# Row numbers through TensorE in two bf16 parts, an earlier scatter, and splits held at the ends of stages, in a two-block fp32 model on one Trainium2 core

## Chip, cores and metric

The kernel runs on one core of one Trainium2 chip. The metric is the device time of one execution in microseconds; lower is better.

## The reference

256 tokens of width 1024, batch 1, all in fp32. The first block has two layers: each a mixer (mLSTM in layer 0, stick-breaking attention in layer 1) and a PEER FFN. A vector c gives, through six matrices per layer (`ada_w`), shift, scale and gate of the mixer and of the FFN. The second block has two layers of half-FFN, attention (MLA, then FOX), half-FFN, and a gated per-layer embedding (PLE).

```python
def first_block(...):
    for layer in range(2):
        sh1, sc1, g1, sh2, sc2, g2 = split(silu(c) @ ada_w[layer] + ada_b[layer], 6)
        h = rmsnorm(x, norm_mix_g[layer]) * (1 + sc1) + sh1
        x = x + g1 * mixer(h)                      # mLSTM | stick-breaking
        h = rmsnorm(x, norm_ffn_g[layer]) * (1 + sc2) + sh2
        x = x + g2 * peer_ffn(h)

def peer_ffn(xb):                                  # 16384 experts, 8 heads, top 16
    s = q(xb) @ sub_keys                           # two lists of 128 scores per head
    s_top, i_top = top_k(s, 16)
    g_top, pos = top_k(s_top[0] + s_top[1], 16)
    expert = (i_top[0] * 128 + i_top[1])[pos]
    act = gelu(dot(peer_u[expert], x))
    return sum(softmax(g_top) * act * peer_v[expert])

def second_block(...):
    for i in range(2):
        h = h + 0.5 * swiglu(rms_norm(h, g_ffn1[i]))
        h = h + attention(rms_norm(h, g_mix[i]))   # MLA | FOX
        h = h + 0.5 * swiglu(rms_norm(h, g_ffn2[i]))
        h = h + sigmoid(rms_norm(h, g_ple[i]) @ w_gate) * (p[i] @ w_proj)
```

## The kernel before

The ten stages follow one another: mLSTM, PEER of layer 0, stick-breaking, PEER of layer 1, FFN, MLA, FFN with PLE, FFN, FOX, FFN with PLE. Weights come from HBM as 1 MB tiles `raw` on SyncE's queue (SP), four of them in flight. For exact fp32 products most weights are split: ScalarE (ACT) rounds a high part `whi` (L228), VectorE (DVE) subtracts it to give `wlo` (L229), and TensorE (PE) does three passes, high×high, low×high, high×low (L277 to L279, L243 to L245). The activations are split alike when the transposes of the next stage's input leave PSUM: `xhi` on ACT, `xlo` on DVE (L320, L321 in `split_T`; L331, L332 with a shift). `split` honours a list `holds`: an entry is a tuple of instructions behind which the next split must stand on the same engine (`issue_after`, an edge in the order, on one engine). A scheduler orders the instructions of each engine by priorities, apart from blocks under `pe_order`, where PE's order is that of the code.

`ada_first` makes the first shift and scale before anything else can run. For the shift, four tiles of `ada_w` go through fp32 matmuls with one output row (L591; each passes twice); the row is turned into columns by eight transposes of one column (L600) and `sh1` is added up (L601). For the scale, four further tiles go through DVE (`ada_scale`, L499), then eight transposes (L517) and sums on ACT (L524). The loads of both alternate.

`peer` serves the first tokens (80 in layer 0, 96 in layer 1) by gathers and the others densely. Dense: `u_phase` multiplies 128 blocks of 1 MB (two experts' rows of 128) of `peer_u` with the tokens (L1443), ACT applies Gelu into X (L1445), a matrix of gates G is built by one-hot products (L1477) and multiplied into X on DVE (L1483), and `v_phase` sums with `peer_v` (L1494). Each of both has two halves of 32 tiles: u0, u1, v0, v1. Gathered: `route` finds the top 16 of 8 heads for 128 tokens; `scatter` spreads the row numbers (`sidx`) and gates (`sg`) to one per partition by four fp32 matmuls with a spreading matrix (L1343), masked products and sums on DVE (L1347, L1349). Then for every four columns one fp32 matmul with the identity carries four row numbers through PE (L1387, held behind the last u or v matmul), ACT casts them to integers (L1389), and GpSimd (POOL) issues one indirect DMA of 128 rows (0.5 MB) per column. DVE takes the dot product (L1399) or adds the weighted row to `sacc` (L1416). The later modulation matrices (`extra`) come in between as ada rows of 0.5 MB and are summed on DVE (L483); at the end a matmul turns a sum into columns (L517, shift or scale) or spreads it (L548, gate `g2b`, after the bias is added on DVE, L546). `par` mixes these generators with the u or v tiles by counts; `route` takes all 16 top-16 steps of the second token block in its turn, so the scheduler may put them ahead of the scatter on DVE.

`last` ends `peer`: per column half two matmuls with `back` bring `sacc` home (L1531), four transposes bring the dense part `oT` (L1534), `residual` multiplies by the gate and adds to x on DVE (L467, L468), and `head` transposes x for the next stage (L303). Attention (`attend`) runs eight head pairs: logits (L928 to L931), exp on ACT (L944), products.

```python
c0, c1, c2 = nf * 27 // 160, nf * 44 // 160, nf * 46 // 160
ne = 14 if l == 0 else 3
par(u0, 12, (rt, 18))
par(u0, half - 12, (rt, 24), (f, c0), (extra, ne))
```

## Time and profile before

| | us |
|---|---|
| median of 3 runs | 2836.63 (2835.41 to 2844.22) |
| profiled execution | 2841.97 |
| its span | 2839.8 |
| PE busy in it | 2740.8 (97%) |
| DVE, ACT, POOL busy | 1938.5 (68%), 929.6 (33%), 450.9 (16%) |
| mean granted PE clock | 0.986 |

The two PEER stages take 177 to 906 and 1064 to 1741 us, more than half of the span. The u and v matmuls alone are busy 604.6 and 608.0 us. A "busy" PE is one with a matmul in flight, at whichever clock; idle time stands with the engine that waits and names what ended the wait.

### The profile page before, as it was taken

Reading aid. Unit: us, or ns where it says so; the run is one execution under the profiler, and the core shown is the slowest. Engines: PE = TensorE matmul, PEld = TensorE weight load, DVE = VectorE, ACT = ScalarE, POOL = GpSimd, SP = SyncE. Lnnn points to the kernel's source line nnn. Section 1 sums busy time; section 2 is a strip of 40 time slices with the busy share of each in tenths; the row PEclk is TensorE's granted clock in tenths of the full one; section 3 lists DMA queues with packets and bytes.
Section 4 is the critical chain, followed back from the end, with each engine's and each line's share of the span. In section 5 each row is a group of like instructions: output and inputs, shape, how many; then the busy total and the mean of one; then the engine's idle time right before and its main releaser. Section 6 shows DMA issues by size and latency. Waiting matters only on the chain.

```text
span 2839.8 us, 47705 instructions
## 1 busy us (share of the span) xinstructions
PE 2740.8 (97%) x19226; PEld 2544.7 (90%) x19226; DVE 1938.5 (68%) x4021; ACT 929.6 (33%) x1730; POOL 450.9 (16%) x445
## 2 busy tenths in 40 slices
PE   7999999999998999999999998999999999999999
PEld 4789989999998779999999987998799989877997
DVE  6778756767645978857777545667766666676665
ACT  4752111100000654111100002446654554456544
POOL 0000332333432000133344431000000000000000
PEclk9999999999999999999999999999999999999999
DMA  7655998999998634799999996554245555452553
GB/s 294 226 179 174 364 372 331 389 359 373 396 407 333 227 118 142 289 401 415 408 408 405 409 409 258 193 186 153 94 169 188 182 179 190 153 175 93 193 191 110
DMA packets 155580, 747.90 MB, mean 263 GB/s; under 512 B 15696, under 2 KB 17360, under 8 KB 111840
## 3 DMA queue, kind: packets, MB, share of 16 engines
q1 hardware_dynamic: 93984, 527.93, 49.9%
q0 software_dynamic: 58752, 213.94, 19.4%
q8 instruction: 151, 2.47, 0.4%
q10 hardware_dynamic: 2624, 3.00, 0.3%
q14 instruction: 69, 0.57, 0.1%
HBM read 743.76 MB, written 1.05 MB: 262 GB/s over the span
## 4 chain that ended last, share of the span: by engine, by line
PE 85%; DMA 7%; DVE 5%; ACT 2%; issue 1%; POOL 0%; SPq 0%; DVEq 0%; ACTq 0%; POOLq 0%
PE ps_acc L1494 17%; PE ps_mm L1443 17%; PE ps_mm L277 7%; PE ps_mm L279 7%; PE ps_mm L278 7%; DMA raw<-in_peer_v_dram 4%; PE ps_acc L244 4%; PE ps_acc L243 4%; PE ps_acc L245 4%; PE ps_acc L1149 3%; PE ps_acc L1151 3%; PE ps_acc L1150 3%; PE ps_mm L1477 1%; DMA raw<-in_ada_w_dram 1%; DVE wlo L229 1%
## 5 line engine op out<-in xcount | busy, mean ns | idle before, releaser
L229 DVE TENSOR_TENSOR wlo<-raw,whi 128x1024 fp32r<-128x1024 f32 (+1 forms) x440 | 532.6, 1214 | 243.4 <-ACT whi L228 232.7
L228 ACT CAST whi<-raw 128x1024 fp32r<-128x1024 f32 (+1 forms) x440 | 456.2, 1042 | 512.2 <-PE ps_mm L278 241.9
L1494 PE MATMUL ps_acc<-X,raw 128*128 128x176 f32 (+1 forms) x4096 | 608.0, 309 | 11.0 <-DMA raw<-in_peer_v_dram 10.8
L1443 PE MATMUL ps_mm<-hT,raw 128*128 128x176 f32 (+1 forms) x4096 | 604.6, 308 | 2.4 <-ACT jT L1673 2.4
L1494 PEld LDWEIGHTS ps_acc<-X,raw 128*128 128x128 f32 x4096 | 587.0, 191 | 16.2 <-DMA raw<-in_peer_v_dram 16.1
L1443 PEld LDWEIGHTS ps_mm<-hT,raw 128*128 128x128 f32 x4096 | 588.6, 191 | 3.4 <-ACT jT L1673 2.6
L277 PE MATMUL ps_mm<-xhi,whi 128*128 128x256 f32 (+1 forms) x1488 | 418.3, 283 | 7.4 <-ACT xhi L332 5.1
L278 PE MATMUL ps_mm<-xlo,whi 128*128 128x256 f32 (+1 forms) x1488 | 418.2, 282 | 3.3 <-DVE xlo L321 3.0
L279 PE MATMUL ps_mm<-xhi,wlo 128*128 128x256 f32 (+1 forms) x1488 | 417.9, 281 | 0.0
L1416 DVE SCALAR_TENSOR_TENSOR sacc<-row,dots,sacc 128x1024 f32<-128x1024 f32 x172 | 220.7, 1283 | 117.2 <-DMA row<-in_peer_v_dram,ix 116.2
L1399 DVE SCALAR_TENSOR_TENSOR row<-row,hn 128x1024 f32<-128x1024 f32 x176 | 213.1, 1224 | 114.7 <-DMA row<-in_peer_un_dram,ix 114.3
L277 PEld LDWEIGHTS ps_mm<-xhi,whi 128*128 128x128 f32 (+1 forms) x1488 | 279.6, 189 | 11.9 <-ACT xhi L332 5.3
L278 PEld LDWEIGHTS ps_mm<-xlo,whi 128*128 128x128 f32 (+1 forms) x1488 | 280.0, 188 | 7.3 <-DVE xlo L321 3.5
L279 PEld LDWEIGHTS ps_mm<-xhi,wlo 128*128 128x128 f32 (+1 forms) x1488 | 281.2, 189 | 0.5 <-DVE wlo L229 0.3
L1392 POOL DMA_INDIRECT row<-in_peer_un_dram,ix x176 | 209.9, 1192 | 446.7 <-ACT ix L1389 156.1
L1392 POOL DMA_INDIRECT row<-in_peer_v_dram,ix x176 | 197.2, 1120 | 340.2 <-ACT ix L1389 177.5
L1445 ACT ACTIVATE X<-ps_mm 128x352 f32<-128x352 f32 (+1 forms) x128 | 57.6, 450 | 495.5 <-PE ps_mm L1443 495.5
L1389 ACT CAST ix<-ps_mm 128x4 int32<-128x4 f32 x88 | 14.2, 161 | 511.8 <-PE ps_mm L1387 440.8
L1483 DVE SCALAR_TENSOR_TENSOR X<-ps_mm,X 128x128 f32<-128x128 f32 (+1 forms) x210 | 66.1, 365 | 125.2 <-PE ps_mm L1477 122.0
L1149 PE MATMUL ps_acc<-whi,ah 128*128 128x512 f32 x352 | 139.4, 396 | 0.0
L1151 PE MATMUL ps_acc<-whi,al 128*128 128x512 f32 x352 | 137.6, 392 | 0.0
L1150 PE MATMUL ps_acc<-wlo,ah 128*128 128x512 f32 x352 | 137.0, 389 | 0.0
(467 smaller groups left out, 3795.1 us busy)
## 6 DMA issues: line engine op xcount, KB each, us to landing
raw<-in_ffn_dram SPq DMA_DIRECT2D x132, 1024.0 KB, 4.8
raw<-in_peer_u_dram SPq DMA_DIRECT2D x128, 1024.0 KB, 7.9
raw<-in_peer_v_dram SPq DMA_DIRECT2D x128, 1024.0 KB, 11.3
raw<-in_ada_w_dram SPq DMA_DIRECT2D x28, 1024.0 KB, 5.4
row<-in_ada_w_dram POOLq DMA_DIRECT2D x40, 512.0 KB, 10.9
raw<-in_peer_wq_dram SPq DMA_DIRECT2D x16, 1024.0 KB, 4.8
raw<-in_fox_in_dram SPq DMA_DIRECT2D x12, 1024.0 KB, 5.1
raw<-in_ma_vo_dram SPq DMA_DIRECT2D x8, 1024.0 KB, 5.6
```

The costliest lines, as they stand in the source:

```text
L228: nc.scalar.copy(hi[:, 0:u], raw)
L229: nc.vector.tensor_sub(lo[:, 0:u], raw, hi[:, 0:u])
L277: nc.tensor.matmul(o, wh, xh[:, k, :], start=(k == 0), stop=False)
L278: nc.tensor.matmul(o, wh, xl[:, k, :], start=False, stop=False)
L279: self.last_mm = nc.tensor.matmul(o, wl, xh[:, k, :], start=False, stop=(k == NK - 1))
L1149: nc.tensor.matmul(o, ah[:, t], wh[:, n], start=(c == 0), stop=False)
L1150: nc.tensor.matmul(o, ah[:, t], wl[:, n], start=False, stop=False)
L1151: nc.tensor.matmul(o, al[:, t], wh[:, n], start=False, stop=(c == FFC - 1))
L1392: nc.gpsimd.indirect_dma_start(row, None, src, bass.IndirectOffsetOnAxis(held["ix"][:, k:k + 1], 0))
L1416: nc.vector.scalar_tensor_tensor(sacc[u], row, w, sacc[u], OP.mult, OP.add)
L1443: self.last_mm = nc.tensor.matmul(ps[:, i * TD:(i + 1) * TD], raw[:, o:o + P], hT[:, k, TS:S], start=(k == 0), stop=(k == NK - 1))
L1494: self.last_mm = nc.tensor.matmul(o, w, xs[:, 0, :], start=(first and c % 2 == 0), stop=last, skip_group_check=True)
```

## The change

In words: (1) `ada_first` sums the scale on PE as well: 16 further fp32 matmuls, all four tiles of the shift loaded first, then four of the scale; DVE's seven sums, the eight 128-column transposes and ACT's sums go. (2) `scatter` carries row number in two parts (row and column of the expert grid) and the gate in one 384-column matmul per unit, two in all; the parts are kept in bf16, and each index pass is two bf16 matmuls that add up in PSUM. (3) The top-16 steps of the second token block stand behind the scatter on DVE; the scatter comes after 7 tiles of u0, held ahead of the next tile's first matmul; u0 takes 33 of 160 gathered columns instead of 27, the later phases fewer, and ada rows go 6, 16, 16, 16 (layer 0) and 0, 3, 3, 3 (layer 1) instead of 14 and 3 in each. (4) `last` transposes `oT` ahead of the `back` matmuls and calls `head` for both halves at the end. (5) `boundary` sets `holds` at the end of every stage with a next one: the first `free` splits behind the last residual add, further ones behind the last evacuation; in `attend` five splits are held behind the exp of head pairs 1 to 5.

```diff
+    def boundary(self):
+        if self.gain is not None:
+            self.holds = [] if self.free == 5 else [(self.add_ins,)] * self.free + [self.evac_ins] * (5 - self.free)
...
@@ ada_first @@
-        scale = self.ada_scale(self.I["ada_w"][0, :, D:2 * D], self.col("ada_b0", 8, 8), self.col("norm_mix_g0"), m["a1"])
+        for e in range(2):
+            for k0 in range(0, NK, 2):
...
+                        nc.tensor.matmul(row[2 * e + h][0:1, :], self.cs[:, k:k + 1], raw[:, o:o + 512], start=(k == 0),
+                                         stop=(k == NK - 1))
...
+                (nc.vector.tensor_copy if h else nc.scalar.copy)(t[0:1, :], row[2 * e + h][0:1, :])
...
@@ mlstm @@
-            self.holds = [(self.sum_ins, self.scale_ins)]
+            self.holds = [(self.tsp_ins,), self.evac_ins, self.evac_ins]
...
@@ attend @@
+            if p in (2, 3, 4, 5, 6):
+                self.holds.append((ex,))
...
@@ peer: tops, scatter @@
+                    with ExitStack() as hold:
+                        if tb:
+                            hold.enter_context(self.tc.issue_after(scattered[-1].ins))
+                        self.top16(rp, s_sb[tb][:, c, :], tv[tb][:, c, :], ti[tb][:, c, :])
...
+                e = rp.tile([P, 3, P], F32, name=f"ex_{l}")
+                nc.scalar.copy(e[:, 2, :], g)
+                nc.vector.tensor_scalar(e[:, 0, :], s0, float(P), float(l * P * P), OP.mult, OP.add)
+                nc.scalar.copy(e[:, 1, :], s1)
...
+                    spread_mm.append(nc.tensor.matmul(ps[:, 0:3 * P], spread[:, u, :], e.rearrange("p a b -> p (a b)"),
+                                                      start=True, stop=True))
...
+                    scattered.append(nc.vector.tensor_reduce(s3[:, :, o:o + n], t4, AX.X, OP.add))
+                    nc.scalar.copy(sidx[:, :, o:o + n], s3[:, 0:2, o:o + n])
...
-                            nc.tensor.matmul(ps[:, 0:PACE], self.ident, sidx[:, col:col + PACE], start=True, stop=True)
+                            for a in range(2):
+                                nc.tensor.matmul(ps[:, 0:PACE], self.identb, sidx[:, a, col:col + PACE],
+                                                 start=(a == 0), stop=(a == 1))
...
+                                if g == 0 and spread_mm and i + k == 0:
+                                    hold.enter_context(self.tc.issue_after(spread_mm[-1].ins))
...
@@ last @@
-                            if tb == 0:
-                                for u in range(2):
-                                    nc.tensor.matmul(ps, back[:, u, :], sacc[u][:, nh * 512:(nh + 1) * 512], start=(u == 0),
-                                                     stop=False, skip_group_check=True)
...
+                            for u in range(0 if tb else 2):
+                                nc.tensor.matmul(ps, back[:, u, :], sacc[u][:, nh * 512:(nh + 1) * 512], start=False,
+                                                 stop=(u == 1), skip_group_check=True)
...
-                        if self.gain is not None:
-                            self.head(nh)
+                    if self.gain is not None:
+                        self.head(0)
+                        self.head(1)
+                        self.boundary()
...
-            c0, c1, c2 = nf * 27 // 160, nf * 44 // 160, nf * 46 // 160
-            ne = 14 if l == 0 else 3
-            par(u0, 12, (rt, 18))
-            par(u0, half - 12, (rt, 24), (f, c0), (extra, ne))
+            c0, c1, c2 = nf * 33 // 160, nf * 43 // 160, nf * 44 // 160
+            ne = 16 if l == 0 else 3
+            par(u0, 7, (rt, 15))
+            next(u0)
+            par(u0, half - 8, (rt, 28), (f, c0), (extra, 6 if l == 0 else 0))
```

`boundary` is called at the end of `tail`, `lin_m` (when `late` is not set) and `last`; `free` is 2 for MLA and FOX, 5 for the FFN ahead of a PLE, 1 elsewhere.

PE in u0 of layer 0, before, around the scatter (L1343) and the first index matmul (L1387); a row with x16 is one tile of `peer_u`, and the first one here is the tenth:

```order
L1443 MATMUL ps_mm_2635<-hT_1607,raw_2636 128x176 x16
L1343 MATMUL ps_mm_2657<-ex_2655,spread_1603 128x128
L1343 MATMUL ps_mm_2666<-r_g_2495,spread_1603 128x128
L1443 MATMUL ps_mm_2687<-hT_1607,raw_2688 128x176 x11
L1343 MATMUL ps_mm_2657<-ex_2655,spread_1603 128x128
L1443 MATMUL ps_mm_2687<-hT_1607,raw_2688 128x176 x5
L1443 MATMUL ps_mm_2719<-hT_1607,raw_2720 128x176 x7
L1343 MATMUL ps_mm_2666<-r_g_2495,spread_1603 128x128
L1443 MATMUL ps_mm_2719<-hT_1607,raw_2720 128x176 x9
L1387 MATMUL ps_mm_2763<-sidx_1562,consts 128x4
```

And with the change (the first row is the seventh tile; L1360 is the scatter, L1408 an index pass):

```order
L1468 MATMUL ps_mm_2575<-hT_1612,raw_2576 128x176 x16
L1360 MATMUL ps_mm_2604<-ex_2600,spread_1608 128x384
L1360 MATMUL ps_mm_2610<-ex_2600,spread_1608 128x384
L1468 MATMUL ps_mm_2616<-hT_1612,raw_2617 128x176 x16
L1408 LDWEIGHTS cb
L1408 MATMUL ps_mm_2648<-sidx_1567,cb 128x4
L1408 LDWEIGHTS cb
L1408 MATMUL ps_mm_2648<-sidx_1567,cb 128x4
```

The four matmuls that stood within tiles ten to twelve are two ahead of the eighth, and the first index pass follows the eighth tile instead of the twelfth. Two to three tiles lie between one index pass and the next in both.

DVE at the end of layer 1's PEER, before, from the copy of the dense sum `oT` on:

```order
L1524 COPY oT_13997<-ps_acc_11877 128x2x160
L229 TENSOR_TENSOR wlo_14167<-raw_14164,whi_14166 128x1024
L1416 SCALAR_TENSOR_TENSOR sacc_1_13548<-row_13974,dots_8588,sacc_1_13548 128x1024
L229 TENSOR_TENSOR wlo_14171<-raw_14164,whi_14170 128x1024
L229 TENSOR_TENSOR wlo_14237<-raw_14234,whi_14236 128x1024
L229 TENSOR_TENSOR wlo_14241<-raw_14234,whi_14240 128x1024
L229 TENSOR_TENSOR wlo_14307<-raw_14304,whi_14306 128x1024
L467 TENSOR_TENSOR tsp_14049<-ps_mm_14042,g2b 128x512
L468 TENSOR_TENSOR x_84<-x_84,tsp_14049 128x512
```

And with the change:

```order
L1549 COPY oT_14081<-ps_acc_11949 128x2x160
L1438 SCALAR_TENSOR_TENSOR sacc_1_13595<-row_14058,dots_8629,sacc_1_13595 128x1024
L473 TENSOR_TENSOR tsp_14133<-ps_mm_14126,g2b 128x512
L474 TENSOR_TENSOR x_84<-x_84,tsp_14133 128x512
L473 TENSOR_TENSOR tsp_14143<-ps_mm_14138,g2b 128x512
L474 TENSOR_TENSOR x_85<-x_85,tsp_14143 128x512
L473 TENSOR_TENSOR tsp_14155<-ps_mm_14148,g2b 128x512
L474 TENSOR_TENSOR x_84<-x_84,tsp_14155 128x512
L473 TENSOR_TENSOR tsp_14165<-ps_mm_14160,g2b 128x512
L324 SCALAR_TENSOR_TENSOR xlo_14171<-ps_mm_14172,cols,xhi_14170 128x256
L474 TENSOR_TENSOR x_85<-x_85,tsp_14165 128x512
L230 TENSOR_TENSOR wlo_14251<-raw_14248,whi_14250 128x1024
```

Five `wlo` splits that stood ahead of the residual adds (L467, L468; now L473, L474) are gone from there; one stands behind the last add, the others behind rows not shown.

PE at the ada shift of layer 0 in u1, before (L1477 is the last product that DVE takes up ahead of the sum, L517 the transposing matmuls):

```order
L1477 MATMUL ps_mm_3796<-B_3740,A_3738 128x64
L1477 LDWEIGHTS A_3738
L1477 MATMUL ps_mm_3796<-B_3740,A_3738 128x64
L1387 MATMUL ps_mm_3814<-sidx_1562,consts 128x4
L517 MATMUL ps_mm_3822<-consts,ada_3283 128x128 x4
L517 MATMUL ps_mm_3828<-consts,ada_3283 128x128 x4
```

And with the change (L1502, L528):

```order
L1502 MATMUL ps_mm_4438<-B_4382,A_4380 128x64
L1408 LDWEIGHTS cb
L1408 MATMUL ps_mm_4456<-sidx_1567,cb 128x4
L1408 LDWEIGHTS cb
L1408 MATMUL ps_mm_4456<-sidx_1567,cb 128x4
L1468 MATMUL ps_mm_4467<-hT_1612,raw_4468 128x176 x16
L528 MATMUL ps_mm_4491<-consts,ada_3782 128x128 x4
L528 MATMUL ps_mm_4497<-consts,ada_3782 128x128 x4
```

One whole tile now stands between that product and the transposes.

## Rows read from the trace of the kernel before

**Rows 1.** Page, busy us (share of the span) and instructions of each engine.

```profile
PE 2740.8 (97%) x19226; PEld 2544.7 (90%) x19226; DVE 1938.5 (68%) x4021; ACT 929.6 (33%) x1730; POOL 450.9 (16%) x445
```

**Rows 2.** Waits of PE: engine, line, releaser: us in total, times, longest.

```profile
PE ps_acc L1494 <- DMA raw<-in_peer_v_dram: 10.8, 24, 2.5
...
PE ps_mm L303 <- DVE x L468: 8.1, 8, 3.0
...
PE ps_mm L548 <- DVE ada L546: 5.6, 1, 5.6
...
PE ps_mm L517 <- DVE ada L483: 4.2, 1, 4.2
PE ps_acc L928 <- ACT e L944: 3.4, 2, 3.1
...
PE ps_mm L303 <- DVE x L1215: 2.6, 1, 2.6
...
PE ps_mm L1443 <- ACT jT L1673: 2.4, 1, 2.4
```

**Rows 3.** Windows, PE: stretch, length, busy (instructions), granted clock, DMA share, GB/s.

```profile
361.10:364.60 3.50, 2.86 (x4) 0.51 1.01 407
443.10:449.90 6.80, 4.86 (x19) 0.50 0.83 291
...
1750.40:1757.20 6.80, 5.53 (x13) 0.50 0.35 145
...
2484.20:2491.10 6.90, 4.59 (x17) 0.51 0.85 302
```

**Rows 4.** Timeline of the start: start, us, engine, line, instruction, count [idle before].

```profile
8.59 5.76 PE L591 MATMUL ps_acc<-raw,cs 128*1 128x512 f32 x8 [8.59 <-ACT cs L1682]
...
21.14 7.03 PE L591 MATMUL ps_acc<-raw,cs 128*1 128x512 f32 x16 [1.65 <-DMA raw<-in_ada_w_dram]
...
30.85 1.28 DVE L499 SCALAR_TENSOR_TENSOR ada<-raw,cs,ada 128x1024 f32<-128x1024 f32 x1
...
38.40 0.79 PE L277 MATMUL ps_mm<-xhi,whi 128*128 128x256 f32 x2 [5.11 <-ACT xhi L332]
```

**Rows 5.** Timeline of layer 0's scatter and first index matmuls, PE and DVE.

```profile
278.04 0.29 DVE L1335 SCALAR_TENSOR_TENSOR ex<-r_sel,r_sel 128x128 f32<-128x128 f32 x1
...
297.38 0.28 PE L1387 MATMUL ps_mm<-sidx,consts 128*128 128x4 f32 x2
297.52 14.57 PE L1443 MATMUL ps_mm<-hT,raw 128*128 128x176 f32 x96
...
306.94 1.22 DVE L1399 SCALAR_TENSOR_TENSOR row<-row,hn 128x1024 f32<-128x1024 f32 x1
...
311.93 0.28 PE L1387 MATMUL ps_mm<-sidx,consts 128*128 128x4 f32 x2
```

**Rows 6.** Groups by line and shape: count, busy us, mean ns, idle before.

```profile
L1477 PE MATMUL ps_mm<-B,A 128*128 128x64 f16 x1344 | 55.1, 193 | 0.0
```

**Rows 7.** Timeline of DVE ahead of the ada shift's sum in u1.

```profile
440.68 0.69 DVE L1483 SCALAR_TENSOR_TENSOR X<-ps_mm,X 128x512 f32<-128x512 f32 x1 [2.92 <-PE ps_mm L1477]
...
443.62 1.27 DVE L483 SCALAR_TENSOR_TENSOR ada<-row,cs,ada 128x1024 f32<-128x1024 f32 x1
```

**Rows 8.** Window of layer 1 (columns as rows 3); page, DMA issues: count, KB, us.

```profile
1207.00:1584.00 377.00, 374.61 (x3231) 1.00 1.02 407
...
row<-in_ada_w_dram POOLq DMA_DIRECT2D x40, 512.0 KB, 10.9
```

**Rows 9.** End of layer 1's PEER: window of PE (columns as rows 3), timeline of DVE.

```profile
1741.04:1762.44 21.40, 12.24 (x56) 0.84 0.49 185
...
1744.81 4.62 DVE L229 TENSOR_TENSOR wlo<-raw,whi 128x1024 fp32r<-128x1024 f32 x4
1749.35 0.69 DVE L467 TENSOR_TENSOR tsp<-ps_mm,g2b 128x512 f32<-128x512 f32 x1
```

**Rows 10.** Timeline of DVE ahead of MLA's first exp.

```profile
1999.24 2.35 DVE L229 TENSOR_TENSOR wlo<-raw,whi 128x1024 fp32r<-128x1024 f32 x2
```

More of the change, by code (lines that the diff above doesn't have):

```diff
@@ L444, in tail @@
             self.head(1)
+            self.boundary()
     def part(self, nb, tb):
@@ L460, in add @@
             if isinstance(gate, float):
-                nc.vector.scalar_tensor_tensor(xs, ps, gate, xs, OP.mult, OP.add)
+                self.add_ins = nc.vector.scalar_tensor_tensor(xs, ps, gate, xs, OP.mult, OP.add)
             elif gate is None:
-                nc.vector.tensor_add(xs, ps, xs)
+                self.add_ins = nc.vector.tensor_add(xs, ps, xs)
             else:
@@ L531, in ada_scale @@
         yield from self.ada_sum(src, bias, sc)
-        self.scale_ins = nc.vector.scalar_tensor_tensor(out, sc, 1.0, g, OP.add, OP.mult)
+        nc.vector.scalar_tensor_tensor(out, sc, 1.0, g, OP.add, OP.mult)
         yield
@@ L577, in ada_first @@
         m = self.mod[0]
-        scale = self.ada_scale(self.I["ada_w"][0, :, D:2 * D], self.col("ada_b0", 8, 8), self.col("norm_mix_g0"), m["a1"])
-        row = [self.ps("acc") for _ in range(2)]
+        row = [self.ps("acc") for _ in range(4)]
         ctx = ExitStack()
-        pool = ctx.enter_context(self.tc.tile_pool(name="first", bufs=3, side="right", reuse_waits="tile"))
-        for k0 in range(0, NK, 2):
-            self.uid += 1
-            end = k0 == NK - 2
-            raw = (self.wpool if end else pool).tile([P, 2048], F32, tag="raw", bufs=4 if end else 3, name=f"raw_{self.uid}")
-            nc.sync.dma_start(raw.rearrange("p (k n) -> p k n", k=2),
-                              self.I["ada_w"][0, k0 * P:(k0 + 2) * P, 0:D].rearrange("(k p) n -> p k n", p=P))
-            for k in range(k0, k0 + 2):
-                for h in range(2):
-                    o = (k - k0) * D + h * 512
-                    nc.tensor.matmul(row[h][0:1, :], self.cs[:, k:k + 1], raw[:, o:o + 512], start=(k == 0),
-                                     stop=(k == NK - 1))
-            if end:
-                ps = self.ps()
-                for h in range(2):
-                    self.uid += 1
-                    t = self.spool.tile([P, 512], F32, tag="tsp", name=f"tsp_{self.uid}")
-                    nc.scalar.copy(t[0:1, :], row[h][0:1, :])
-                    for c in range(4):
-                        nc.tensor.transpose(ps[:, h * 4 + c:h * 4 + c + 1], t[0:1, c * P:(c + 1) * P], self.ident[0:1, 0:1])
-                nc.vector.tensor_add(m["sh1"], ps[:, 0:NK], self.col("ada_b0", 0, NK))
-            if k0 < 4:
-                next(scale, None)
@@ L604, in ada_first @@
-        for _ in scale:
-            pass
+        pool = ctx.enter_context(self.tc.tile_pool(name="first", bufs=4, side="right", reuse_waits="tile"))
+        for e in range(2):
+            for k0 in range(0, NK, 2):
+                self.uid += 1
+                raw = (self.wpool if e else pool).tile([P, 2048], F32, tag="raw", bufs=4, name=f"raw_{self.uid}")
+                nc.sync.dma_start(raw.rearrange("p (k n) -> p k n", k=2),
+                                  self.I["ada_w"][0, k0 * P:(k0 + 2) * P, e * D:(e + 1) * D].rearrange("(k p) n -> p k n", p=P))
+                for k in range(k0, k0 + 2):
+                    for h in range(2):
+                        o = (k - k0) * D + h * 512
+                        nc.tensor.matmul(row[2 * e + h][0:1, :], self.cs[:, k:k + 1], raw[:, o:o + 512], start=(k == 0),
+                                         stop=(k == NK - 1))
+            ps = self.ps("acc" if e else "mm")
+            for h in range(2):
+                t = pool.tile([P, 512], F32, tag=f"row{e}{h}", bufs=1, name=f"row{e}{h}")
+                (nc.vector.tensor_copy if h else nc.scalar.copy)(t[0:1, :], row[2 * e + h][0:1, :])
+                for c in range(4):
+                    nc.tensor.transpose(ps[:, h * 4 + c:h * 4 + c + 1], t[0:1, c * P:(c + 1) * P], self.ident[0:1, 0:1])
+            b = self.col("ada_b0", 8 * e, 8)
+            if e:
+                sc = self.small(NK, "adas")
+                nc.vector.tensor_add(sc, ps[:, 0:NK], b)
+                nc.vector.scalar_tensor_tensor(m["a1"], sc, 1.0, self.col("norm_mix_g0"), OP.add, OP.mult)
+            else:
+                nc.vector.tensor_add(m["sh1"], ps[:, 0:NK], b)
@@ L1329, in peer @@
             chosen = {}
+            spread_mm, scattered = [], []
             def scatter():
                 g, s0, s1 = chosen[0]
[L1334 to L1350 removed]
```

70 lines of the change are left out of this document (36 added, 34 removed).

## The prediction, made before the change had run

> **What bounds the kernel now.** I read the busy shares first: TensorE (PE) is busy 2740.8 of 2839.8 us [rows 1]. So the matmuls set the time, and a change that leaves their count almost alone can only win or lose in the 99 us in which PE stands still and in the stretches at half clock behind those stops. The waits of PE come next [rows 2]: no wait is long, the largest is 10.8 us in 24 pieces. The change must therefore be costed wait by wait. The third view, windows laid over the stretch right after a stop, shows the second half of the price [rows 3]: the granted clock stands at 0.50 for 3.5 to 6.9 us (1.2 GHz instead of 2.4), so half of the PE busy time in such a window is lost too: 1.4, 2.4, 2.8 and 2.3 us in the four windows shown.
>
> 0.3% of the time is 8.5 us; less than that I call no change.
>
> **The start.** All eight loads of the first modulation now end in PE sums: 64 matmuls instead of 32. The first eight took 5.76 us, the last sixteen 7.03 us, or 0.44 us each [rows 4]. From 8.59 us: 5.76 + 56 × 0.44 = 30.4, with the transposes that stand in between and the small chain behind (copy, eight transposes, add, scale, evacuation, cast; some 4 us) the first projection matmul starts at about 43.5 us instead of 38.40. Before, the DVE sum ended at 30.85 + 1.28 = 32.1 us [rows 4], under the loads. So **+5 us**, bounds +2 (PE goes on without the slow first matmuls) to +8. SP loads the same eight blocks ahead of the next weights; what is behind them doesn't move.
>
> **Index matmuls.** The fp32 pass costs PE the step from 297.38 to 297.52, 0.14 us [rows 5]. The nearest rows for two bf16 passes with their weight loads are the 1344 16-bit matmuls of L1477: 55.1 us, 41 ns each [rows 6]. So 0.14 - 0.08 = 0.06 us, 40 times in layer 0 and 48 times in layer 1. Layer 1 goes by DMA (below), so I count **-2 us**, bounds 0 and -5. The Trainium skill (TensorE: Matmul & The Clock Gate, section LDWEIGHTS (loading the stationary operand)) gives a weight load of 128 columns 107 ns; by that two loads would cost 0.21 us and the 88 passes 6 us more instead of less. The 41 ns for load and matmul together speak against it, since the loads overlap; the sum doesn't use it.
>
> **Scatter and gathers in layer 0.** Before, the row numbers were formed on DVE at 278.04, yet the first index matmul stood after 12 blocks of the u pass, at 297.38 [rows 5]. Blocks cost (311.93 - 297.38) / 3 = 4.85 us. The change puts the scatter after block 7 and the first index matmul after block 8: 4 × 4.85 = 19 us sooner. PE would come to the scatter at 297.38 - 5 × 4.85 = 273.1, and DVE was ready at 278.04 + 0.29; but part of the DVE work ahead of it (top-16 steps of the second token block) now stands behind it: some 25 short operations, at 0.2 to 0.29 us each (the row that forms the numbers) 5 to 7 us. So the wait is between 0 and 5.2 us; I take 1. ScalarE (ACT) now has the Gelu of the first 16 dot products in front of the exp of the second routing and of the next evacuations, so it waits there for row 16. That row's index matmul is three blocks, 14.6 us, ahead; a first row took 306.94 - 297.38 = 9.6 us [rows 5], three more some 1.5 us each. Behind ACT stand the next index cast and the evacuations; PE has two more PSUM tiles, 9.7 us, before it waits. I take 1 us, bounds 0 and 8 per layer. Together **+2 us**.
>
> **The two ada waits in layer 0.** PE waited 5.6 us for the last sum of the gate (L548) and 4.2 us for that of the shift (L517) [rows 2], and lost 1.4 and 2.4 us of clock behind them [rows 3]. Why, shows DVE: its stream waited until 440.68 for a PE product that stands right in front of L517 on PE, then had 4.2 us of work up to the end of the sum at 443.62 + 1.27 [rows 7]. In the new order the shift's matmuls stand a whole block (4.85 us) behind such a product, with nearly the same DVE operations between, some 4.6 us: the wait goes, **-6.5 us**, or nothing if rows come late. The gate's matmuls move from after block 24 to after block 36; there DVE has about 7 us to do against 4.9 of PE, so some 2 us stay: **-5 us**, bounds -7 and -1.
>
> **Layer 1.** From 1207 to 1584 the DMA engines moved 407 GB/s without a break [rows 8], and PE's waits in the v pass are all for its blocks [rows 2]. There bytes set the time. By 1207 the index groups of 20 rows are out instead of 12; a row tile is 0.5 MB [rows 8], less three ada rows that move behind: 8 × 0.5 - 1.5 = 2.5 MB, at 407 GB/s **-6 us**. Bounds: -14, if all of 10.8 and 2.4 us (the wait for jT) go; +3, if the 1.5 MB that come into the last v phase cost what they weigh (3.7 us).
>
> **Stage ends.** At the end of layer 1 PE's last v block ended at 1741.04, and the next stage's first matmul came at 1762.44; in these 21.4 us PE was busy 12.24 us, at a mean clock of 0.84 [rows 9]. DVE ran four low-part splits, 4.62 us, ahead of the residual adds [rows 9]. Now one split stands between the adds, the rest behind the last evacuation; the transposes of oT fill the wait for the last row. DVE needs 8 × 0.69 for four gated adds [rows 9]; with the last row ahead of them and transposes and xlo behind, some 3 to 4 us each, 12 to 14 us are left: **-8 us**, bounds -11 and -3. In MLA five splits (2.35 us for two [rows 10]) leave the path to the first exp and go between the head pairs, where PE was never idle; PE waited 3.4 us for exp [rows 2], with a stretch at half clock behind it like those of [rows 3]: **-5 us**, bounds -8 and -1. FOX's start: the window holds 2.3 us of standstill and 2.3 of clock [rows 3]: **-4.5 us**, bounds -7 and 0. The gate of the first PLE into the next FFN: 2.6 us [rows 2] of which the splits are part, -2.5; three further ends -1.5: **-4 us**, bounds -8 and 0. If a held split comes late instead, PE waits for wlo, 1.2 us each.
>
> **The sum:** +5 - 2 + 2 - 6.5 - 5 - 6 - 8 - 5 - 4.5 - 4 = -34 us. The profiled execution took 2841.97 us, so it would be 2808; the median of the runs is 5.3 us lower, 2836.63, which gives **2803 us**. With the bounds taken as independent its own range is 2791 to 2817.
>
> **Rivals.**
> *The chain, not the splits, sets the stage ends.* Add, square, transpose, cast follow each other, and a held split only moves behind them. Speaks for it: PE waits there for x (L468), not for a split [rows 2]. Against: the splits stand in front of that x on DVE [rows 9]. Then a third of the 21.5 us of stage ends comes: -34 + 14.5, 2817 us. Chance 0.18.
> *Layer 1 stays bound by DMA.* Blocks wait for bytes; the earlier gathers fill buffers that were full anyway, and 1.5 MB more come late: +3 instead of -6, 2812 us. For it: 407 GB/s for 377 us. Against: PE waited only 10.8 us. The Trainium skill (DMA: Bandwidth & Descriptors, section Where 436 GB/s comes from) holds that the HBM side binds at about 358 GB/s; by that rule nothing PE saves in layer 1 comes out. The trace goes past that figure for 377 us, so I don't lean on it further. Chance 0.10.
> *It doesn't do what it says.* The edges act on one engine only, and other work of DVE and ACT takes the place of the splits: stage ends -5, ada shift wait back (0), layer 1 0, start +8, row waits +4: -2 - 5 + 4 - 5 + 8 = 0, 2837 us. Chance 0.10.
> *Slower: the scatter comes before DVE is ready.* If the moved top-16 steps give DVE nothing back, PE waits 5.2 us at the scatter and loses 1.5 of clock; and if row 16 comes 18 us later than three blocks cover, ACT's held evacuations stop PE for 18 - 9.7 = 8 us and 1.5 of clock: 16 us, in each of two layers. The late rows also keep the ada waits, and layer 1 gives nothing. 32 + 8 (start) - 2 - 21.5 = +16.5, **2853 us**. It decides from about 8 us per layer on. Against it: those DVE steps do move. Chance 0.08.
>
> **The numbers.** The forecast has 0.54, the rivals 0.18, 0.10, 0.10 and 0.08. Faster by over 0.3%: 0.54 + 0.18 + 0.10 = 0.82; within: 0.10; slower: 0.08. The range 2788 to 2832 takes in the forecast with its bounds, the first two rivals and the near side of the third.
>
> **What would show it.** PE's waits for DVE ada at L559 and L528 under 3 us together; the first index matmul near 280 us; waits for x at L474 after the last v block under 3 us together; waits for e (L956) under 1 us; first L280 matmul at 42 to 46 us; DMA waits of the v pass (L1519) between 3 and 8 us. Wrong it is if PE waits at L1360 or for Gelu evacuations by more than 5 us, or if waits for wlo appear at stage starts.

## The result, and the profile after

The changed kernel takes 2854.27 us (median of 5 runs, 2852.44 to 2861.24), the kernel before 2837.10 beside it: ratio 1.0059, 95% interval 1.0041 to 1.0077. It is 17 us slower, where 34 us less were forecast. The profiled execution took 2852.44 us (span 2850.7), 10.5 us above that of before, which lies 5 us above its own median.

The page, engines (answers to [rows 1]):

```profile
PE 2754.4 (97%) x19250; PEld 2537.3 (89%) x19250; DVE 1931.0 (68%) x4005; ACT 929.4 (33%) x1728; POOL 433.2 (15%) x445
```

PE has 13.6 us more of busy time and about as much idle time as before: waits went and others came. The waits of PE (answers to [rows 2]; L559 and L528 were L548 and L517, L474 was L468):

```profile
PE ps_acc L1519 <- DMA raw<-in_peer_v_dram: 10.0, 21, 2.3
...
PE ps_mm L280 <- DVE sg L1182: 7.4, 4, 2.2
PE ps_acc L423 <- DVE rrt L422: 6.9, 2, 4.5
PE ps_mm L1360 <- ACT ex L1355: 6.5, 2, 4.6
...
PE ps_mm L1468 <- ACT jT L1700: 4.3, 1, 4.3
PE ps_mm L306 <- DVE x L474: 3.2, 5, 1.2
...
PE ps_mm L559 <- DVE ada L557: 2.2, 1, 2.2
...
PE ps_acc L938 <- ACT e L956: 1.3, 2, 0.9
...
PE ps_mm L528 <- DVE ada L494: 0.7, 2, 0.4
```

Gone are 9.8 - 2.9 = 6.9 us for ada, 4.9 for x at L474, 2.1 for the exp. New are sg and rrt (the norm of the next stage: `rrt` is its last DVE product, `sg` the first use of it in an FFN) and ex (the scatter's operand), 20.8 us together. The stretches behind the new stops, with the old gate stop first (stretch, length; busy us and instructions of PE, PEld, DVE, ACT, POOL; granted clock, DMA share, GB/s):

```profile
361.00:364.60 3.60, 3.60 (x28) 3.55 (x27) 3.60 (x11) 0.52 (x2) 2.43 (x2) 1.00 1.01 393
...
279.20:284.50 5.30, 3.38 (x12) 2.83 (x12) 3.79 (x10) 1.24 (x4) 0.00 (x0) 0.81 0.59 202
1150.50:1158.50 8.00, 3.44 (x8) 2.18 (x8) 5.62 (x10) 1.03 (x3) 0.00 (x0) 0.65 0.37 131
...
1740.07:1751.50 11.43, 9.29 (x58) 6.83 (x56) 9.03 (x17) 6.47 (x16) 0.00 (x0) 1.00 0.44 171
1751.50:1763.90 12.40, 12.05 (x96) 11.47 (x96) 12.40 (x46) 7.81 (x11) 0.00 (x0) 1.00 0.58 207
1763.90:1775.30 11.40, 5.98 (x31) 5.65 (x31) 7.14 (x39) 5.99 (x13) 0.00 (x0) 0.70 0.37 145
```

The end of layer 1 is 11.4 us long instead of 21.4 [rows 9] and at full clock, as intended; 12.4 us later PE stands still, and the mean clock of the next 11.4 us is 0.70. To see where time goes I compare marks: the start of the same matmul in two profiled executions. Each column says how much longer (+) or shorter the stretch is than in the profile of before, in us:

| stretch, up to | after | c1 | b1 | e1 | e2 | e7 | e8 | e12 |
|---|---|---|---|---|---|---|---|---|
| u pass of layer 0 | +7.1 | +6.7 | -0.4 | +8.9 | +6.0 | +6.8 | +0.2 | +0.4 |
| its block 16 (scatter) | +3.6 | +3.6 | 0.0 | +3.5 | -0.4 | +3.6 | -0.4 | -0.4 |
| its block 24 (old gate stop) | -9.1 | -9.1 | +1.4 | -9.1 | -9.1 | -9.1 | -9.1 | -9.1 |
| u pass of layer 1 | -7.2 | -0.6 | -0.6 | -4.2 | -3.8 | -7.7 | -4.2 | -0.6 |
| its block 16 (scatter) | +7.0 | +7.1 | 0.0 | +7.2 | -0.2 | +7.2 | -0.2 | -0.3 |
| its last v matmul | -2.1 | -1.6 | -1.1 | -3.0 | -0.9 | -5.1 | +0.2 | -6.9 |
| end of the first FFN | -0.9 | -1.1 | +2.1 | -5.2 | -1.0 | -5.8 | -4.6 | -5.9 |
| second product of the FFN behind MLA | +0.8 | +0.8 | +1.0 | -0.1 | +0.8 | -2.4 | -2.4 | -2.4 |
| the same behind the first PLE | +3.6 | +3.5 | +1.9 | +0.1 | +3.6 | -1.2 | -0.5 | -1.2 |
| the same behind FOX | +8.4 | +8.7 | +9.7 | +0.3 | +8.7 | +3.6 | -2.4 | -0.9 |
| end of the span | +10.9 | +17.7 | +13.9 | -2.0 | +3.8 | -10.3 | -23.2 | -27.1 |

The other columns are the experiments. Equal code repeats within 2 us from run to run, but for the first row (3 us), the fourth (10) and the sixth (6).

### The profile page after: what moved, and what is told of

Read it like the earlier page. It is cut to its first block, busy times and chain, and to the rows that moved or that the text cites. A ratio compares the mean times of both kernels' runs of the same rounds, so it can differ in the third digit from the quotient of the medians.

```text
span 2850.7 us, 47773 instructions
## 1 busy us (share of the span) xinstructions
PE 2754.4 (97%) x19250; PEld 2537.3 (89%) x19250; DVE 1931.0 (68%) x4005; ACT 929.4 (33%) x1728; POOL 433.2 (15%) x445
## 4 chain that ended last, share of the span: by engine, by line
PE 68%; DMA 17%; DVE 9%; issue 3%; ACT 2%; POOL 1%; ACTq 0%; DVEq 0%; POOLq 0%
PE ps_acc L1519 11%; PE ps_mm L280 7%; PE ps_mm L282 7%; PE ps_mm L281 7%; PE ps_mm L1468 6%; DMA raw<-in_peer_v_dram 5%; DMA row<-in_peer_un_dram,ix 5%; DMA row<-in_peer_v_dram,ix 4%; PE ps_acc L245 4%; PE ps_acc L244 4%; PE ps_acc L246 4%; PE ps_acc L1161 3%; PE ps_acc L1163 3%; PE ps_acc L1162 3%; DMA row<-in_ada_w_dram 2%
## 5 line engine op out<-in xcount | busy, mean ns | idle before, releaser
L280 PE MATMUL ps_mm<-xhi,whi 128*128 128x256 f32 (+1 forms) x1488 | 422.7, 284 | 11.4 <-DVE sg L1182 7.4
L1414 POOL DMA_INDIRECT row<-in_peer_un_dram,ix x176 | 199.3, 1132 | 588.0 <-DVE ti L1619 240.1
L1414 POOL DMA_INDIRECT row<-in_peer_v_dram,ix x176 | 190.1, 1080 | 337.0 <-ACT ix L1411 171.1
L1470 ACT ACTIVATE X<-ps_mm 128x352 f32<-128x352 f32 (+1 forms) x128 | 57.5, 451 | 482.0 <-PE ps_mm L1468 384.9
```

The source lines that it names most:

```text
L280: nc.tensor.matmul(o, wh, xh[:, k, :], start=(k == 0), stop=False)
L1414: nc.gpsimd.indirect_dma_start(row, None, src, bass.IndirectOffsetOnAxis(held["ix"][:, k:k + 1], 0))
```

## The experiments

**c1, the changed kernel once more.**

> The changed kernel itself once more, so that it stands beside the repaired ones on the same chip. Its layer 0 from block 24 of the u pass to the first v block took 4.4 us less than before in its first profile, but 0.6 to 2.1 us more in two experiments that leave that stretch as it is. Theory A (that stretch varies from run to run, and the first profile caught a good one): span 2852 to 2858 and median 2853 to 2858. Rival B (the experiments changed it): the first profile is repeated within 1.5 us at each mark.

Measured: 2856.89 us (ratio 1.0053, 1.0033 to 1.0073), span 2857.5. Theory A: only the fourth row differs, by 6.6 us. There PE waits for the gate's sum (L559) for 4.8 us instead of 2.2, which explains 2.6 of them; where the other 4 go is not shown. The first profile, the fastest of its five runs, had caught a good one; that is why it shows 11 us and the medians 17.

**e1, no holds.** `boundary` leaves the list empty, `attend` appends nothing:

```diff
-            self.holds = [] if self.free == 5 else [(self.add_ins,)] * self.free + [self.evac_ins] * (5 - self.free)
+            self.holds = []
...
-            if p in (2, 3, 4, 5, 6):
-                self.holds.append((ex,))
```

> The changed kernel with no split held at stage ends (boundary leaves the list empty) and none in the attention pairs; everything else of the change stays. Theory A (held splits land on DVE among the steps of the next stage's norm chain, so that rrt, rrow and sg come late and PE stops a few microseconds into the next stage): the waits of PE for rrt (L422) and for sg (L1182) go back to under 1 us together, the stages behind the first FFN give back about 12 us, and the total is about 2842 us. Rival B (the holds are harmless; what the stage ends lost comes from the other order in last, from the second pass of the index matmuls or from the clock): no change, 2851 to 2857. Rival C (the holds are worth what the prediction said and something else hides it): slower by 10 to 20 us.

Measured: 2834.22 us (0.9969, 0.9951 to 0.9986), span 2837.8. Theory A, and more than it said: the four stage-end rows of the table add up to -5.0 us, against +11.9 in the changed kernel. By these rows the holds cost 17 us; no wait for rrt or sg is left in the list. What the holds were meant for goes with them: x at L474 is awaited 6.1 us again and the exp 3.4. The ratios of e1 and c1 differ by 24 us; the further 7 us lie outside the stage ends and are not explained.

**b1, the holds alone, in the kernel before** (part 5 of the change, nothing else).

> The kernel before with part (5) of the change alone: boundary and the holds in attention, everything else as before. Theory A (the holds cost, wherever they stand): FFN starts behind MLA, PLE and FOX lose 3.3, 3.6 and 4.5 us and FOX's attention 4.6 us, MLA's start gives 2 to 3 us back, the boundary into the first FFN gives nothing; total 10 to 15 us slower than before, about 2850. Rival B (they cost only together with the other order in last or with the earlier scatter): within 4 us of before. Rival C (they pay, as the prediction says): 10 us or more faster.

Measured: 2855.27 us (1.0059, 1.0038 to 1.0080): as slow as the whole change. Its column is nearly empty up to layer 1 (1.4 us at most), and behind the first FFN it follows that of the change; the waits for sg are the same 7.4 us, those for rrt 5.5. Theory A: 13 us by the medians.

**e7, the norm chain goes first.** One split behind the last add (two ahead of MLA and FOX), one behind the last evacuation, six behind the last rrt:

```diff
-            self.holds = [] if self.free == 5 else [(self.add_ins,)] * self.free + [self.evac_ins] * (5 - self.free)
+            self.chain = []
+            self.holds = [] if self.free == 5 else [(self.add_ins,)] * self.free + [self.evac_ins] + [self.chain] * 6
...
+            self.chain.append(rrt)
```

> The changed kernel with one further edge at the stage ends: one split behind the last residual add, one behind the last evacuation, and the next six behind the two products rrt that end the norm chain. Theory A (the splits between the steps of the norm chain are what delays sg): the first FFN keeps its earlier start (first projection matmul about 11 us ahead of before) and its first second-stage matmul is 8 to 10 us ahead of before instead of 1.7; the waits for rrt and sg fall below 1.5 us together; the other stage ends give 2 to 4 us; total about 2840. Rival B (DVE has too little room for both, so the splits come late instead): waits for wlo or whi of 5 us and more, no change. Rival C (the chain is late for another reason, the rotary tables or the squares on ACT): waits for sg unchanged.

Measured: 2837.74 us (0.9981, 0.9964 to 0.9998), span 2829.5. Theory A in the main. In the changed kernel DVE's timeline at the start of the first FFN reads (L353 to L355 are the steps of the chain; rotary tables left out):

```profile
1754.39 1.22 DVE L230 TENSOR_TENSOR wlo<-raw,whi 128x1024 fp32r<-128x1024 f32 x1
...
1755.60 0.15 DVE L353 TENSOR_TENSOR nw<-st 128x2 f32<-128x2 f32 x1
...
1755.99 1.22 DVE L230 TENSOR_TENSOR wlo<-raw,whi 128x1024 fp32r<-128x1024 f32 x1
1757.13 0.15 DVE L354 TENSOR_TENSOR nw<-nw,nw 128x2 f32<-128x2 f32 x1
1757.20 1.22 DVE L230 TENSOR_TENSOR wlo<-raw,whi 128x1024 fp32r<-128x1024 f32 x1
...
1758.67 1.22 DVE L230 TENSOR_TENSOR wlo<-raw,whi 128x1024 fp32r<-128x1024 f32 x1
1759.81 0.15 DVE L355 SCALAR_TENSOR_TENSOR st<-nw,st 128x2 f32<-128x2 f32 x1
1759.88 1.22 DVE L230 TENSOR_TENSOR wlo<-raw,whi 128x1024 fp32r<-128x1024 f32 x1
...
1768.10 0.48 DVE L422 TENSOR_SCALAR rrt<-consts,st 128x128 f32<-128x128 f32 x2
```

Eight splits of 1.22 us stand between steps of 0.15 us, and PE, whose next instruction is the product with rrt, waits for the end of the chain:

```profile
1768.44 1.22 PE L423 MATMUL ps_acc<-rrt,consts 128*128 128x128 f32 x4 [4.50 <-DVE rrt L422]
1770.58 0.58 PE L280 MATMUL ps_mm<-xhi,whi 128*128 128x256 f32 x1 [0.92 <-DVE sg L1182]
```

With the chain first, DVE in e7 (its stage starts 3.5 us sooner; L423 is rrt, L231 wlo, L354 the chain):

```profile
1750.87 1.22 DVE L231 TENSOR_TENSOR wlo<-raw,whi 128x1024 fp32r<-128x1024 f32 x1
1752.08 0.15 DVE L354 TENSOR_TENSOR nw<-st 128x2 f32<-128x2 f32 x1
...
1756.62 0.47 DVE L423 TENSOR_SCALAR rrt<-consts,st 128x128 f32<-128x128 f32 x2
1757.01 4.62 DVE L231 TENSOR_TENSOR wlo<-raw,whi 128x1024 fp32r<-128x1024 f32 x4
```

rrt comes 11.5 us sooner, 8.0 of them counted from its own stage's start, and the splits still come in time: PE waits 0.9 us for wlo in two pieces (L283), 0.3 in the changed kernel. The waits for sg at the three later FFN starts, 2.2 us each, are gone. The chain is not out of the way altogether: PE still waits 1.7 us for rrt at the first FFN and 1.3 at FOX, where the changed kernel has 4.5 and 2.4, so the two waits together stay above the 1.5 us that A named:

```profile
PE ps_acc L424 <- DVE rrt L423: 3.0, 2, 1.7
```

**e5, no splits held in FOX's attention** (`and qs is not None` in the condition of `attend`).

> The changed kernel with no splits held in the attention of FOX; those of MLA and of the stage ends stay. In the run without any holds FOX's attention lasted 4.6 us less up to the next projection, and the stage behind it 4.8 us less. Theory A (the five splits between the head pairs delay FOX's own DVE and ACT work, so that PE waits there): the 1.4 us inside the attention and the 3.2 us behind it come back, 4.6 us; the 4.5 us lost at the start of the last FFN stay, since that is the norm chain; total about 2849. Rival B (only the edges at the stage end cost): no change, 2854. Rival C (the splits that are no longer held go in front of the attention): its start comes 3 us later and the total is the same.

Measured: 2849.84 us (1.0033, 1.0019 to 1.0046). Theory A for the size: FOX's row falls from +8.4 to +3.5. Its mechanism was wrong: PE stands still for hardly any of it (8.9 us in all on the stretch of that row, 8.4 in e5). The timeline of PE in the changed kernel shows the values' products of one pair of heads (L828, L830, two passes each, 64 columns of the array per head):

```profile
2599.14 0.65 PE L828 MATMUL ps_mm<-a,v 128*64 128x256 f32 x2
2599.72 0.33 PE L816 MATMUL ps_mm<-consts,e 128*128 128x128 f32 x1
...
2603.51 0.32 PE L830 MATMUL ps_mm<-a,v 128*64 128x128 f32 x1
2603.51 0.43 PE L828 MATMUL ps_mm<-a,v 128*64 128x256 f32 x1
...
2604.31 0.44 PE L818 MATMUL ps_mm<-consts,e 128*128 128x128 f32 x2
```

and in e5:

```profile
2601.70 0.66 PE L828 MATMUL ps_mm<-a,v 128*64 128x256 f32 x4
2602.18 0.40 PE L830 MATMUL ps_mm<-a,v 128*64 128x128 f32 x4
2602.51 0.33 PE L816 MATMUL ps_mm<-consts,e 128*128 128x128 f32 x1
```

In e5 both heads run side by side, four passes of 0.4 us in 0.48, the whole pair in 0.81 us. In the changed kernel the first head's wide product goes ahead of the next pair's transposes, alone (0.58 us), and the rest takes 0.80: 0.57 us more. That is so in seven of FOX's eight pairs, in one before: 6 x 0.57 = 3.4 of the 4.9 us. This is read from the traces; no run changes the order of the products alone, and that the held splits bring it about by delaying the DVE copy behind the narrow products is my reading. Of the remaining 1.5 us the idle time is 0.5; the rest is not explained.

**e2, the scatter after 9 blocks** (`par(u0, 9, (rt, 15))`, `half - 10` behind it).

> The changed kernel with the scatter after 9 blocks of u0 instead of 7. Theory A (PE comes to the scatter before DVE and ACT have its operand, 1.9 us in layer 0 and 4.6 us in layer 1, and then runs at half clock): PE's wait for ex falls below 0.5 us in both layers, about 5 us come back in layer 0 and 8 us in layer 1, less what later rows cost; total about 2843 us. Rival B (the second block's top-16 steps behind the scatter, or the wider matmul, cost the time wherever it stands): no change, 2852 to 2857. Rival C (rows that come 10 us later bring the ada waits back): ada waits of over 2 us, total 2850 or more.

Measured: 2850.83 us (1.0034, 1.0020 to 1.0048). Theory A for the wait: it is gone, and the two scatter rows go from +3.6 and +7.0 to -0.4 and -0.2. In the changed kernel PE and ACT at the scatter of layer 1:

```profile
1154.76 0.30 ACT L1355 COPY ex<-r_sel 128x128 f32<-128x128 f32 x1 [3.74 <-DVE r_sel L1683]
...
1155.11 2.93 PE L1360 MATMUL ps_mm<-ex,spread 128*128 128x384 f32 x4 [4.56 <-ACT ex L1355]
```

in e2:

```profile
1157.38 1.45 PE L1360 MATMUL ps_mm<-ex,spread 128*128 128x384 f32 x4
```

The routing on DVE ends when it ends; two blocks later PE doesn't see it, and the same matmuls take half. Of the 11 us in the two rows about 7 show in the medians' difference (1.0059 to 1.0034).

**e3 and e9, the start.** e3 is the changed kernel with `ada_first` and the first holds of before:

> The changed kernel with the start of the kernel before (first scale summed on DVE, its hold of the first splits). Theory A (16 more fp32 matmuls are on the path that sets the start): the first projection matmul comes back to 38.4 us and the first mlstm product to about 68, total down by 7 to 9 us, about 2846. Rival B (part of the delay is made up later, since the background ada rows run on DVE and arrive whenever the start ends): the start gains 6 to 9 us but layer 0 gives half of it back, 2850.

Measured: 2851.24 us (1.0023, 1.0008 to 1.0038): the first projection matmul at 37.90 us instead of 44.98, 8 to 10 us in the ratio, 7 at the mark. The profiled run was the slowest of ten, so what layer 0 gives back can't be read from it. e9 has the other three repairs of e8 (below) with the new start:

> The four repairs without that of the start: the scale is summed on PE, as in the change. Theory A (the new start costs its 6.6 us and layer 0 gives back 3 to 4 of them, since the background ada rows and the gathers are then less late): 3 to 7 us slower than with all four, 2826 to 2830. Rival B (nothing is given back): 7 us or more. Rival C (all of it is given back): the same.

Measured: 2831.60 us (0.9968, 0.9957 to 0.9979), 8.6 us above e8. Both say: the start costs its 7 us or a little more, and nothing is given back (theory A of e3, Rival B of e9). PE's share of it, in the changed kernel:

```profile
8.78 19.35 PE L601 MATMUL ps_acc<-raw,cs 128*1 128x512 f32 x40 [8.78 <-ACT cs L1709]
...
38.07 3.59 PE L601 MATMUL ps_acc<-raw,cs 128*1 128x512 f32 x8
...
44.98 0.39 PE L280 MATMUL ps_mm<-xhi,whi 128*128 128x256 f32 x1 [2.14 <-ACT xhi L337]
```

**e4, one fp32 index matmul again** (both parts added on DVE behind the scatter).

> The changed kernel with the two parts of a row number added on DVE right behind the scatter and one fp32 index matmul for four columns, as before the change. Theory A (the two bf16 passes are worth 0.06 us each, as the prediction counts): the u and v passes of layer 0 grow by 40 x 0.06 = 2.4 us, those of layer 1 by less than 3 us, total up by 2 to 5 us on the changed kernel, 2855. Rival B (the second weight load costs more than the fp32 pass saves): 3 to 6 us faster, 2849. Rival C (too small to see): the spans between the first index matmul and the end of each layer agree within 1 us.

Measured: 2857.98 us (1.0052, 1.0035 to 1.0069), the same as c1. Inconclusive in the total; in the first half of layer 0's v pass, with 11 index groups, the two kernels differ by 1.6 us, 0.145 us a group in favour of bf16; in the next three eighths of that pass, with 8 groups, by 0.7 us, 0.09 a group. The loads show it, before (L1387) and after (L1408), min/median/max ns:

```profile
L1387 PEld LDWEIGHTS ps_mm<-sidx,consts x176: 188/190/193, 297.2 to 1717.9; 128*128 128x128 f32 x176
```

```profile
L1408 PEld LDWEIGHTS <-cb x176: 96/98/98, 288.8 to 1717.6; 128*128 128x128 bf16 x176
```

An fp32 pass loads twice, so both kernels have 176 loads; those in bf16 take half as long.

**e6, the counts of before** (27, 44, 46; ada rows 14 and 3 in each phase).

> The changed kernel with the counts of before (27, 44, 46 of 160 gathered columns; 14 or 3 ada rows in each of the four phases). Theory A (the two ada waits of layer 0 go because the counts move their matmuls, as the prediction says): PE's waits for ada rise from 2.9 to 8 us or more, layer 0 loses 8 to 13 us, layer 1 loses less than 6, total 2864. Rival B (the earlier scatter alone removes the waits, since the rows come earlier): ada waits stay under 4 us and the total within 3 us of the changed kernel.

Measured: 2863.59 us (1.0072, 1.0055 to 1.0089). Theory A in layer 0: the third row is +4.4 instead of -9.1, PE waits 8.9 us for the gate and 4.5 for the shift. But layer 1's sixth row is -7.3, better than with the new counts.

**e8, four repairs together:** start of before, scatter after 9 blocks, norm chain first, no holds in FOX's attention.

> The changed kernel with four repairs together: the start of before, the scatter after 9 blocks, the splits of a stage end behind the norm chain, no held splits in FOX's attention. If the four causes are separate, as theory A says, the gains by the marks of the single runs add up, on the profiled spans: start 3 to 7, scatter 12 less 3 to 5 that the v phase of layer 1 gives back, norm chain 21, FOX 4.6: about 36 us below the changed kernel, 2816 us, and 20 us below the kernel before. Rival B (the v phase of layer 1 and the ada sums take up what is gained ahead of them): 2824 to 2830.

Measured: 2823.03 us (0.9943, 0.9923 to 0.9963), span 2816.6. The profiled execution is the fastest of the four, so that it meets A's 2816 is luck; by the ratios e8 is 31 us below c1, between A's 36 and the 21 to 27 of B. By the marks each repair works: -9.9 us at the four stage ends, -0.4 and -0.2 at the scatters, +0.2 at the start. **e10** is e8 without any hold:

> Start of before, scatter after 9 blocks, and no holds at all, neither at stage ends nor in attention. Theory A (behind the norm chain the holds are worth something: against the run without holds, 2.4, 1.2 and 2.4 us at the starts of the three later FFNs, 0.8 in MLA's attention, nothing at the first FFN, where the other order in last gives all of the gain): 5 to 8 us slower than the four repairs, about 2829. Rival B (the norm chain only undoes the harm): the same as the four repairs within 2 us in the marks.

Measured: 2829.39 us (0.9963, 0.9949 to 0.9977), 6.4 us more (5.7 by the ratios). The two intervals overlap; the four stage-end rows add up to -5.5 instead of -9.9, so that by the marks the holds are worth 4.4 us once the norm chain goes ahead of them: theory A, a little under its 5 to 8. At the end of layer 1 they are worth nothing: the row of the first FFN is -4.8 without any hold (-5.2 in e1), -4.6 with them, and +2.1 with holds and the old order in `last` (b1). So the gain there is not that of the holds; what is left for it is the new order, part (4), which no run has alone. **e14** is e8 without those in MLA's attention:

> The four repairs together, with no splits held in MLA's attention either; the stage ends stay. Theory A (holds in attention let the first product of a pair of heads go ahead alone, so that two heads no longer run side by side, as FOX's trace shows; five lone pairs of 0.6 us in MLA against three without): MLA's attention loses the 3.1 us it gained by a shorter way to the first exp, but not the 1.5 us behind it: 1.5 to 2 us slower over the stage, 2825. Rival B (they cost as in FOX): 1 to 3 us faster.

Measured: 2827.24 us (0.9945, 0.9925 to 0.9964). The ratios can't be told apart; MLA's row (second product of the FFN behind it) is +1.8 instead of -2.4, and PE waits 3.4 us for exps instead of 1.3. So there the holds pay 4.2 us, more than A said: the splits really leave the way to the first exp. With no holds at the stage ends either, the row is -0.5 (e10); no run shows why holds at the stage ends alone are worse than none.

**e12 and e13, layer 1's counts.** e12 is e8 with both old counts in layer 1, e13 with only its three ada rows back in u0:

> The four repairs together, and in layer 1 the counts of before (27, 44, 46 of 160 gathered columns, three ada rows in each phase). Theory A (more gathers in u0 of layer 1 fill the DMA engines there and are paid back by late blocks): layer 1 from block 16 of u0 to the last v block takes 4 to 7 us less than with the four repairs, total about 2818. Rival B (layer 1 is bound by its bytes, whatever the order): within 2.5 us, which is how far equal code differs from run to run there.

> The four repairs together, with three of layer 1's ada rows in u0 as before instead of behind it; the gathers as in the change. Theory A (it is the 1.5 MB of ada rows that arrive in the last v phase, 3.7 us by bytes): layer 1 gains 3 to 4 us, as much as with all old counts. Rival B (it is the gathers, or nothing): within 2.5 us.

Measured: e12 2818.93 us (0.9927, 0.9910 to 0.9943), the lowest median of all, 21 us under the kernel before; e13 2823.77 (0.9941, 0.9925 to 0.9958). The interval of e12 overlaps that of e8. The sixth row is -6.9 in e12, +0.2 in e8, -2.6 in e13: by this mark theory A of e12, and e6, which also has the old counts behind the earlier scatter, has -7.3; five runs with the new counts and the scatter at 9 lie between -3.2 and +2.5. But with the new counts and the scatter at 7 this row reaches -5.7 (e5), so the old counts are probably better and by how much stays open. e13 settles nothing. PE's waits behind block 16 of layer 1, in e8:

```profile
PE ps_acc L1523 <- DMA raw<-in_peer_v_dram: 10.4, 20, 1.9
PE ps_mm L1472 <- ACT jT L1704: 3.6, 1, 3.6
PE ps_mm L1472 <- DVE X L1512: 3.5, 1, 3.5
```

and in e12:

```profile
PE ps_acc L1523 <- DMA raw<-in_peer_v_dram: 13.5, 30, 2.5
PE ps_mm L1472 <- DVE X L1512: 0.2, 1, 0.2
```

The new counts load u0, and PE stops twice in the u pass, for ACT (`jT`) and for DVE (`X`); with the old ones almost only blocks that have not landed are left. In both kernels the DMA engines are busy on the whole stretch of that row, at 403 and 407 GB/s (windows of e8, then of e12, columns as in the windows above):

```profile
1183.30:1727.30 544.00, 526.56 (x4325) 518.74 (x4324) 359.97 (x674) 33.60 (x110) 205.41 (x191) 0.99 1.01 403
...
1186.90:1723.80 536.90, 523.19 (x4327) 514.17 (x4325) 359.29 (x676) 33.53 (x111) 212.67 (x192) 1.00 1.02 407
```

## Why the prediction was wrong, point by point

**Stage ends, -21.5 forecast, +12 measured: the step that failed.** It held that the splits move behind the last evacuation at no other price than "if a held split comes late instead, PE waits for wlo, 1.2 us each". The first half came true: the end of layer 1 is 10 us shorter, x is awaited 3.2 us instead of 8.1, the exp 1.3 instead of 3.4. The price went elsewhere. No split came late to speak of (PE's waits for wlo are 2.8 us in all, 2.2 before); what came late was the norm chain, a dozen dependent steps of 0.15 us that now share DVE's queue with eight held splits of 1.22 us. I asked who waits for the held split and not what is queued behind it. e1 and b1 show the cost of the holds from both sides, e7 where most of it sits. Even with the chain first the stage ends give about -10 us (e8, e12), of which -5.5 come without any hold (e10). FOX's second part, products that no longer run side by side, was in no term at all.

**The marks it named.** The first projection matmul at 42 to 46 (44.98) and x at L474 behind the last v block (1.2 of the 3.2 us, for 3) came true; ada waits under 3 us did in the first profile (2.9) and not in c1 (6.2); the exp (1.3 for 1) nearly; the first index matmul (288.8 for 280) and the v pass's DMA waits (10.0 for 3 to 8) did not; waits at L1360 above 5 us (6.5) were named as a sign of error.

**The rivals.** "The chain, not the splits" gave a third of the gain to the stage ends; with the chain first that is about the truth: -5.8 in e7, -9.9 in e8. "Slower" landed on the time (2853), mostly by luck. PE did wait at the scatter, 1.9 and 4.6 us where it had 5.2 each. In layer 1 PE also stopped at evacuations: ACT waited 9.7 us for the Gelu of the first 16 dot products (L1425), with the routing's copies and a block's evacuation (L1470) behind it, and PE stood for 4.3 us. The rival had 8 in each layer; c1 has 2.4, as the kernel before had at this wait. Timelines of ACT and PE in the changed kernel:

```profile
1226.26 0.22 ACT L1425 ACTIVATE dots<-dots 128x16 f32<-128x16 f32 x1 [9.65 <-DVE row L1421]
...
1229.63 2.77 PE L1468 MATMUL ps_mm<-hT,raw 128*128 128x160 f32 x9 [4.34 <-ACT jT L1700]
...
1230.89 0.44 ACT L1470 ACTIVATE X<-ps_mm 128x320 f32<-128x320 f32 x1
```

Of its 32 us in the two PEER layers the scatter rows show 10.6, and its -21.5 at the stage ends came out at +12: two errors that cancel. "It doesn't do what it says" is not the reason: the edges held, as the shorter waits for x and the exp show.

**Scatter, +2 forecast, +10.6 measured.** The wait was bounded at 0 to 5.2 us and I took 1 for layer 0 and none for layer 1, where it is 4.6. The clock behind it (0.81 and 0.65) was in the rival alone.

**Start, +5 forecast, +7 measured:** right, within the bounds.

**Index matmuls, -2 forecast:** right in sign. 0.09 to 0.145 us a group, 40 groups, is an estimate of -3.6 to -5.8 in layer 0, about at the bound of -5; the total does not show it. The Trainium skill (TensorE: Matmul & The Clock Gate, section LDWEIGHTS (loading the stationary operand)) has a weight load take its columns divided by 1.2, in ns, an estimate of 107 ns for 128; the trace has 98 ns for bf16 and 190 for each fp32 load. By its rule, set against one 0.14 us step as I did it, the change would lose; what my comparison left out is that the fp32 matmul loads twice.

**The ada waits, -11.5 forecast:** right in mechanism. The gate's stop gives -9.1 with the new counts (-7.9 in e4) and +4.4 in e6; the moved gate waits 2 to 8 us from run to run, and the shift 3.8 us again in e14, so the sum up to the v pass is -13.5 in the first profile and -7.5 in c1.

**Layer 1, -6 forecast, +5 measured.** 7 us of it are the scatter. The rest is probably the opposite of what I wrote: in the sixth row the two runs with the earlier scatter and the old counts (e6, e12) gain 7 us, and the new counts, which I counted as part of the gain, take some or all of it back. The rival "bound by DMA" isn't refuted: the DMA engines are busy in e8 as in e12, and the stretch is 1% shorter where the rate is 1% higher. In e12 407 GB/s flow for 537 us, with one core running, which speaks again against the 358 GB/s that the Trainium skill (DMA: Bandwidth & Descriptors, section Where 436 GB/s comes from) holds to bind.

## What to carry to other kernels

Work that is moved off one critical path lands in the queue of another: before holding it, list what follows on the same engine, and look for short dependent chains there, since each step of such a chain can let one long instruction in. An edge that holds work should name the last instruction of the next chain, not only of the one it protects. Judge such a change by marks, stage by stage: here -10 us at the end of layer 1 and +9 us in the first FFN lay 25 us apart and added up to -0.9.

## What the runs showed of the hardware

Matmuls of 64 columns on different halves of the array ran side by side where they stood next to each other in PE's order: at most 15 ns apart in start, 0.81 us a pair of heads instead of 1.38. The Trainium skill (TensorEngine Tiling (Array Packing), section Tiling Modes) says that such tiles execute independently; the trace agrees, and adds that one product sent ahead alone loses it. A scatter of four passes took 1.45 us at full clock (e2) and 2.93 behind a stop of 4.6 us, where the granted clock was 0.65 over the 8 us of stop and scatter. And equal code in the PEER passes differed by up to 10 us between profiles, more than most terms of the sum.
